# Every two-operand operation that a planner shares out between VectorE and GpSimd goes to VectorE

## The chip, the cores and the metric

The kernel runs on one core of one Trainium2 chip. The metric is the time of one execution on the device in microseconds (us); lower is better. Engines are named as in the profile: PE is TensorE, DVE is VectorE, ACT is ScalarE, POOL is GpSimd, SP the queue that issues most transfers.

## What is computed

Two layers of a transformer trunk over 512 latent tokens and 256 context tokens, width 1024, all in float32. Layer 0 mixes with two kinds of attention over latents (a window, and a 2-D neighbourhood with bias), each latent also reading all context keys; layer 1 with multi-head latent attention (low-rank queries, keys and values, a separate rotary part). Each layer ends in a squared-ReLU MLP of width 4096. Cut to what matters:

```
for i in range(2):
    sh1, sc1, g1, sh2, sc2, g2 = split(silu(c) @ ada_w[i] + ada_b[i], 6)
    h_lat = rms_norm(x, norm_mix[i]) * (1 + sc1) + sh1          # the same for ctx with c_ctx
    y_lat, y_ctx = even_mixer(h_lat, h_ctx, ...) if i % 2 == 0 else odd_mixer(h_lat, h_ctx, ...)
    x = x + g1 * y_lat
    h2 = rms_norm(x, norm_mlp[i]) * (1 + sc2) + sh2
    x = x + g2 * (square(relu(h2 @ mlp_w1[i])) @ mlp_w2[i])     # ctx too in layer 0
return x
```

## The kernel before

**Arithmetic.** A float32 product is made of three fp32r products. An operand is split into a high part (a copy to fp32r: names wh, hh, uh, oh) and a low part, source minus high part (wl, hl, ul, ol); `mm3` adds wh·h, wh·l and wl·h in PSUM. So each weight tile of 128x1024 that arrives by DMA (raw) needs one copy and one subtraction before PE can use it: `split`, called by `Weights.pump` for 128 tiles of the MLPs (wl_w) and for those of the projections (wl_qa, wl_kqb, wl_vb, wl_eo, wl_oi, wl_kv, wl_uq, wl_oo). There are three buffers each for raw, high and low tiles. `split` also makes the low parts of the MLP's activations (ul), of the attention outputs (ol, oh, D) and of latent factors (lr, kb).

**Stages.** Up to 50 us the first modulation; from 50 to about 410 us the first layer's attention (`mixer0`, tiles with _a, _b, _qa, _kqb, _vb in their names); then its output projection (ps_eo) and MLP, to 1060 us; from 1060 to 1390 us the second layer's attention (`mixer1`: 8 pairs of heads, four query jobs `UQ` and eight key-and-value jobs `KV`; tiles with _c, _kv, _uq); then ps_oo and the second MLP. In the MLPs the order is fixed by loops. In the attention stages generators (gemms, their preparation, scores, values, projection) are interleaved by `weave`, which keeps a model of each engine's clock (`Clock`) and always continues the generator whose next PE work could begin first by that model. The schedule is manual: every engine runs its instructions in exactly the order in which this host program emits them, so an instruction that waits holds back all behind it on its engine.

**Who does what.** Three helpers choose an engine by that model when an operation is emitted. `pick` sends a copy to ACT or DVE, `square` a square to ACT or POOL, and `pick2` an operation with two operands in SBUF to POOL or DVE, whichever would end first. `pick2` serves the subtraction in `split` (unless an engine is given, as for three early weight tiles), `scale_by` (normalised queries and keys times 1/rms: ur, oT, qr, kr) and one multiplication by a gain (rows_sb). Other uses of POOL are written out: six additions of squares per norm (nsq). In an attention score half, DVE finds row maxima (mx) and combines them (nm, 128x2), ACT takes the exponential (P), PE transposes P (pp) and multiplies by the values (o).

Of the kernel before, what the change touches and what calls it, by code (L numbers as in the profile page):

```python
# [272 lines left out]
def hybrid_block(  # L273
# [32 lines left out]
    pe, act, dve, pool = (Engine(e, n, ck) for e, n in (  # L306
        (nc.tensor, "pe"), (nc.scalar, "act"), (nc.vector, "dve"), (nc.gpsimd, "pool")))
# [133 lines left out]
    def pick2(n):  # L441

        d = ck.t["dve"] + 0.07 + n / 960
        p = ck.t["pool"] + 0.3 + 2.3 * n / 1000
        return pool if p < d else dve

    def split(hi, lo, src, eng=None):
        copy(hi, src, False)
        (eng or pick2(src.free_size())).tensor_tensor(lo, src, hi.bitcast(F32), op=ALU.subtract)
# [518 lines left out]
    def scale_by(r, y):  # L968

        pick2(r.free_size()).tensor_tensor(r, r, y[:, :, None].to_broadcast(list(r.shape)), op=ALU.mult)  # L970
# [13 lines left out]
    def mixer0(hh, hl, ap, oT, proj, first):  # L984
# [24 lines left out]
        class Unit(Job):  # L1009
# [37 lines left out]
            def prep(self, M):  # L1047
# [17 lines left out]
                for b in range(3):  # L1065
                    scale_by(hd(self.r[b]), box[0][:, b * n2:(b + 1) * n2])
                    if grow is not None:
                        x = hd(self.r[b])
                        pick2(x.free_size()).tensor_tensor(x, x, grow[:, None, :].to_broadcast(list(x.shape)),
                                                           op=ALU.mult)  # L1070
# [1162 lines left out]
```

## Time and profile before

| | |
|---|---|
| time, median of 3 runs | 1787.21 us (1785.69 to 1788.28) |
| the profiled execution's own time | 1784.65 us |
| its span | 1782.8 us |
| PE busy | 1713.3 us, 96% of the span |
| DVE busy | 1030.3 us, 58%, 1908 instructions |
| ACT busy | 653.6 us, 37% |
| POOL busy | 454.3 us, 25%, 241 instructions |

The profile gives the busy time of each engine, and the same by stretches of time. PE's share is an average of stages: in the MLPs it is busy without a break, in the two attention stages it is not. Each group of instructions has a count, a mean duration and the idle time of its engine just before it. An instruction's duration here includes time in which it has begun and is held up by another engine's access.

### The profile page before, as it was taken

The page shows a single profiled execution, that of the slowest core. Times are in us where ns is not written, and L with a number is a line of the kernel's source. Part 1 is how long each engine was busy: PE and PEld are TensorE (multiplying, and loading weights), DVE is VectorE, ACT ScalarE, POOL GpSimd, SP SyncE. Part 2 cuts the span into 40 slices and gives each one's busy share as a digit, 9 for nine tenths or more (in the row PEclk, how much of TensorE's full clock was granted, in tenths as well). Part 3 has the DMA queues.
Part 4 walks back from the last instruction along what each step waited for, and adds up shares of the span by engine and source line. Part 5 has one row for each costly group of instructions (what it writes and reads, how often), then busy time and mean ns, then how long its engine had stood idle before and what let it go on. Part 6 is the DMA issues. An engine that isn't in the chain of part 4 may idle for free. (4 is left out here: it accounts for less than half of the span.)

```text
span 1782.8 us, 27692 instructions
## 1 busy us (share of the span) xinstructions
PE 1713.3 (96%) x11304; PEld 1471.5 (83%) x11304; DVE 1030.3 (58%) x1908; ACT 653.6 (37%) x1403; POOL 454.3 (25%) x241
## 2 busy tenths in 40 slices
PE   9999998989999999999999997999999999999999
PEld 7987876858888888888888896777676898989897
DVE  6767766474667686444445557868864652414242
ACT  3445555343232132132132233555554241414141
POOL 0232111021233332333333222302110233242422
PEclk9999999999999999999999998999999999999999
DMA  9311113043324334343342210001000233323332
GB/s 304 112 60 60 37 48 125 28 142 118 95 84 134 126 118 151 122 130 119 129 127 86 80 47 31 26 1 36 24 13 1 83 107 95 94 90 94 93 94 83
DMA packets 49663, 158.21 MB, mean 89 GB/s; under 512 B 7777, under 2 KB 10209, under 8 KB 49409
## 3 DMA queue, kind: packets, MB, share of 16 engines
q1 hardware_dynamic: 48192, 154.96, 27.4%
q8 instruction: 89, 1.46, 0.3%
q10 hardware_dynamic: 1344, 1.49, 0.3%
q14 instruction: 38, 0.30, 0.1%
HBM read 154.32 MB, written 2.11 MB: 88 GB/s over the span
## 5 line engine op out<-in xcount | busy, mean ns | idle before, releaser
L131 PE MATMUL p<-hh_m,wh_w 128*128 128x258 f32 (+2 forms) x1024 | 317.9, 310 | 0.3 <-DVE fr_m L131 0.3
L131 PE MATMUL p<-hl_m,wh_w 128*128 128x258 f32 (+2 forms) x1024 | 317.9, 310 | 0.0
L131 PE MATMUL p<-hh_m,wl_w 128*128 128x258 f32 (+2 forms) x1024 | 317.7, 310 | 0.0
L131 PE MATMUL p<-ul,wh_w 128*128 128x512 f32 (+1 forms) x768 | 273.1, 356 | 0.0
L131 PE MATMUL p<-uh,wh_w 128*128 128x512 f32 (+1 forms) x768 | 272.2, 354 | 0.0
L131 PE MATMUL p<-uh,wl_w 128*128 128x512 f32 (+1 forms) x768 | 271.7, 354 | 0.0
L131 ACT ACTIVATE wh_w<-raw_w 128x1024 fp32r<-128x1024 f32 x114 | 120.1, 1058 | 397.7 <-PE p L131 383.7
L131 POOL TENSOR_TENSOR wl_w<-raw_w,wh_w 128x1024 fp32r<-128x1024 f32 x65 | 164.9, 2538 | 318.3 <-ACT wh_w L131 263.4
L131 PEld LDWEIGHTS p<-hh_m,wl_w 128*128 128x128 f32 x1024 | 193.4, 189 | 11.1
L131 PEld LDWEIGHTS p<-hh_m,wh_w 128*128 128x128 f32 x1024 | 192.9, 188 | 11.7 <-DVE fr_m L131 0.5
L131 PEld LDWEIGHTS p<-hl_m,wh_w 128*128 128x128 f32 x1024 | 193.1, 189 | 11.2
L131 DVE SCALAR_TENSOR_TENSOR dots<-dot_raw,dots 128x1024 f32<-128x1024 f32 x80 | 148.1, 1851 | 39.6 <-DMA dot_raw<-in_ada_t_dram 38.7
L131 DVE SCALAR_TENSOR_TENSOR x<-p,mod,x 128x512 f32<-128x512 f32 x96 | 60.3, 658 | 189.0 <-PE p L131 189.0
L131 POOL TENSOR_TENSOR ul<-u,uh 128x512 fp32r<-128x512 f32 (+1 forms) x52 | 99.6, 1916 | 258.6 <-DVE uh L131 258.6
L131 PEld LDWEIGHTS p<-uh,wh_w 128*128 128x128 f32 x768 | 145.2, 189 | 21.2
L131 PEld LDWEIGHTS p<-uh,wl_w 128*128 128x128 f32 x768 | 145.0, 189 | 20.9
L131 PEld LDWEIGHTS p<-ul,wh_w 128*128 128x128 f32 x768 | 145.1, 189 | 20.7 <-DVE ul L131 0.2
L131 DVE TENSOR_TENSOR wl_w<-raw_w,wh_w 128x1024 fp32r<-128x1024 f32 x63 | 96.7, 1536 | 100.7 <-ACT wh_w L131 100.4
L131 DVE CAST uh<-u 128x768 fp32r<-128x768 f32 (+1 forms) x64 | 32.7, 510 | 97.7 <-ACT u L131 97.7
L131 ACT ACTIVATE r<-r,bs_p 128x256 f32<-128x256 f32 x64 | 39.5, 617 | 103.9 <-DVE r L131 101.1
L131 PEld LDWEIGHTS pp_c<-ident,P 128*128 128x128 f32 x384 | 46.7, 151 | 26.6 <-issue 14.6
L131 PE MATMUL pp_c<-ident,P 128*128 128x128 f32 x384 | 58.3, 296 | 7.9 <-DVE kb L131 3.1
(494 smaller groups left out, 3472.3 us busy)
## 6 DMA issues: line engine op xcount, KB each, us to landing
raw_w<-in_mlp_w_dram SPq DMA_DIRECT2D x128, 512.0 KB, 3.6
dot_raw<-in_ada_t_dram SPq DMA_DIRECT2D x56, 512.0 KB, 3.7
ada_raw<-in_ada_w_dram SPq DMA_DIRECT2D x24, 512.0 KB, 4.5
ada_raw<-in_ada_s_dram SPq DMA_DIRECT2D x16, 512.0 KB, 10.2
raw_kqb<-in_e_w_in_dram SPq DMA_DIRECT2D x8, 512.0 KB, 3.6
raw_eo<-in_e_w_out_dram SPq DMA_DIRECT2D x8, 512.0 KB, 4.0
raw_oo<-in_o_w_out_dram SPq DMA_DIRECT2D x8, 512.0 KB, 3.4
raw_oi<-in_o_w_in_dram SPq DMA_DIRECT2D x6, 512.0 KB, 3.6
```

Source lines behind the costliest of these rows:

```text
L131: r = f(*a, **k)
```

## The change

`pick2` returns DVE whatever its model says. The model's two estimates are still worked out and no longer used.

```
@@ -442,7 +442,7 @@
 
         d = ck.t["dve"] + 0.07 + n / 960
         p = ck.t["pool"] + 0.3 + 2.3 * n / 1000
-        return pool if p < d else dve
+        return dve
 
     def split(hi, lo, src, eng=None):
         copy(hi, src, False)
```

In the order of the instructions this takes 195 operations from POOL to DVE. In the second attention stage after 1080 us they are 32: 13 scalings qr (8 of 512 columns, 5 of 256), 7 scalings kr (768), 5 wl_kv (3 of 896, 2 of 512), 2 wl_oo (1024), 4 low parts of the attention output (512) and kb (768). In the first one, between 50 and 410 us, they are 35: 14 weight splits (1024), 4 ol (768), 17 scalings (15 of 512, 2 of 256). Most of the others are in the MLPs (65 wl_w and 52 ul). POOL keeps the 18 norm additions and the squares. Because `weave`, `pick` and `square` read the model's clocks, other things move with it: 41 single-operand copies go from DVE to ACT, and 12 squares from ACT to POOL (24 squares there before, 36 now). In the second attention stage these are 22 copies, net, and 8 squares (8 before, 16 now); in the first about 12 copies and 4 squares (16 before, 20 now). PE runs the same instructions; in the first attention stage they come in a visibly different order, in the second nearly in the same one.

DVE at the opening of the second attention stage, where the raw queries of the first `UQ` job (two tiles qr, each 128x768 with 8 heads of 64 plain and 32 rotary columns) are multiplied by 1/rms (y) and rotated (tu). Before:

```order
L131 TENSOR_TENSOR y_uq_10411<-y_uq_10404,w_uq_10407 128x32
L131 TENSOR_TENSOR qr_uq_10154<-qr_uq_10154,y_uq_10411 128x8x32
L131 TENSOR_TENSOR qr_uq_10154<-qr_uq_10154,rows_sb 128x8x32
L131 TENSOR_TENSOR tu_uq_10416<-qr_uq_10154,ropeq 128x256
L131 TENSOR_TENSOR tu_uq_10416<-qr_uq_10154,ropeq 128x16x8 x2
L131 TENSOR_TENSOR qr_uq_10154<-tu_uq_10416 128x8x32
L131 TENSOR_TENSOR qr_uq_10196<-qr_uq_10196,rows_sb 128x8x32
L131 TENSOR_TENSOR tu_uq_10424<-qr_uq_10196,ropeq 128x256
```

The same place now:

```order
L131 TENSOR_TENSOR y_uq_10411<-y_uq_10404,w_uq_10407 128x32
L131 TENSOR_TENSOR qr_uq_10154<-qr_uq_10154,y_uq_10411 128x8x64
L131 TENSOR_TENSOR qr_uq_10154<-qr_uq_10154,y_uq_10411 128x8x32
L131 TENSOR_TENSOR qr_uq_10154<-qr_uq_10154,rows_sb 128x8x32
L131 TENSOR_TENSOR tu_uq_10416<-qr_uq_10154,ropeq 128x256
L131 TENSOR_TENSOR tu_uq_10416<-qr_uq_10154,ropeq 128x16x8 x2
L131 TENSOR_TENSOR qr_uq_10154<-tu_uq_10416 128x8x32
L131 TENSOR_TENSOR qr_uq_10196<-qr_uq_10196,y_uq_10411 128x8x64
L131 TENSOR_TENSOR qr_uq_10196<-qr_uq_10196,y_uq_10411 128x8x32
L131 TENSOR_TENSOR qr_uq_10196<-qr_uq_10196,rows_sb 128x8x32
L131 TENSOR_TENSOR tu_uq_10424<-qr_uq_10196,ropeq 128x256
```

Three multiplications by y that POOL did beside DVE now stand in DVE's own row, two of them with 8x64 columns per partition.

DVE late in the first attention stage, at the last normalisation of neighbourhood queries and keys (three tiles ur_kqb; w and y are the steps to 1/rms), between the first tiles of the output projection (wl_eo, oh, ol) and a piece of the modulation (mod). Before:

```order
L131 TENSOR_TENSOR w_kqb_4317<-y_kqb_4305 128x24
L131 TENSOR_TENSOR w_kqb_4317<-w_kqb_4317,v_kqb_4300 128x24
L131 TENSOR_SCALAR w_kqb_4317<-w_kqb_4317 128x24
L131 TENSOR_TENSOR y_kqb_4321<-y_kqb_4305,w_kqb_4317 128x24
L131 CAST oh_4356<-oT 128x768
L131 TENSOR_TENSOR ol_4357<-oT,oh_4356 128x768
L131 TENSOR_TENSOR ur_kqb_4075<-ur_kqb_4075,y_kqb_4321 128x512
L131 TENSOR_TENSOR ur_kqb_4209<-ur_kqb_4209,y_kqb_4321 128x512
L131 TENSOR_TENSOR wl_eo_4384<-raw_eo_4315,wh_eo_4383 128x1024
L131 TENSOR_TENSOR mod_107<-ada_pt_4391,adab_sb 128x16 x2
L131 TENSOR_TENSOR ol_4357<-oT,oh_4356 128x768
L131 SCALAR_TENSOR_TENSOR k_kqb_4372<-ut_kqb_4415,gains_sb,k_kqb_4371 64x512
```

The same place now:

```order
L131 TENSOR_TENSOR wl_eo_4288<-raw_eo_4243,wh_eo_4287 128x1024
L131 TENSOR_TENSOR w_kqb_4293<-y_kqb_4281 128x24
L131 TENSOR_TENSOR w_kqb_4293<-w_kqb_4293,v_kqb_4276 128x24
L131 TENSOR_SCALAR w_kqb_4293<-w_kqb_4293 128x24
L131 TENSOR_TENSOR y_kqb_4297<-y_kqb_4281,w_kqb_4293 128x24
L131 TENSOR_TENSOR ur_kqb_3977<-ur_kqb_3977,y_kqb_4297 128x512
L131 TENSOR_TENSOR ur_kqb_4168<-ur_kqb_4168,y_kqb_4297 128x512
L131 TENSOR_TENSOR ur_kqb_4257<-ur_kqb_4257,y_kqb_4297 128x512
L131 TENSOR_TENSOR ol_4340<-oT,oh_4339 128x768 x2
L131 SCALAR_TENSOR_TENSOR k_kqb_4336<-ut_kqb_4359,gains_sb,k_kqb_4335 64x512
```

The weight split wl_eo, the third scaling and the low parts ol that POOL did are now in DVE's row; the three scalings stand right behind y, and the modulation no longer stands between them and the transposed keys (k_kqb<-ut_kqb).

POOL through the first three groups of jobs of the second attention stage, 143 to 150 of its row before, sq being squares:

```order
L131 TENSOR_TENSOR sq_uq_10691<-qr_uq_10376 128x768
L131 TENSOR_TENSOR sq_uq_10695<-qr_uq_10542 128x768
L131 TENSOR_TENSOR wl_kv_10704<-raw_kv_10323,wh_kv_10703 128x512
L131 TENSOR_TENSOR qr_uq_10376<-qr_uq_10376,y_uq_10769 128x8x64
L131 TENSOR_TENSOR qr_uq_10376<-qr_uq_10376,y_uq_10769 128x8x32
L131 TENSOR_TENSOR qr_uq_10542<-qr_uq_10542,y_uq_10769 128x8x64
L131 TENSOR_TENSOR qr_uq_10542<-qr_uq_10542,y_uq_10769 128x8x32
L131 TENSOR_TENSOR sq_kv_10864<-kr_kv_10580 128x768
```

The same jobs now:

```order
L131 TENSOR_TENSOR sq_kv_10429<-kr_kv_10248 128x768
L131 TENSOR_TENSOR sq_kv_10485<-kr_kv_10328 128x768
L131 TENSOR_TENSOR sq_uq_10608<-qr_uq_10381 128x768
L131 TENSOR_TENSOR sq_uq_10627<-qr_uq_10545 128x768
L131 TENSOR_TENSOR sq_kv_10878<-kr_kv_10586 128x768
```

Only squares are left there, among them those of KV jobs that ACT did before.

## Rows read from the trace of the kernel before

**Rows 1.** The view by stretches: start and end in us, length, then busy us (and instructions) of PE, PE's weight loads, DVE, ACT and POOL, granted PE clock as a share of full speed, DMA share and GB/s.

```profile
50.00:410.00 360.00, 332.43 (x2708) 275.52 (x2707) 248.17 (x585) 169.63 (x512) 77.17 (x51) 0.99 0.23 73
410.00:1060.00 650.00, 649.09 (x3806) 572.79 (x3805) 371.78 (x530) 174.94 (x242) 197.51 (x78) 1.00 0.36 114
1080.00:1390.00 310.00, 279.92 (x1849) 218.35 (x1849) 217.31 (x463) 161.21 (x428) 54.21 (x39) 0.93 0.06 18
1390.00:1783.00 393.00, 388.98 (x2439) 351.93 (x2438) 144.94 (x236) 120.34 (x173) 120.94 (x66) 1.00 0.31 94
```

**Rows 2.** The chain that ended last, by engine as shares of the span, and its first piece (start us, us, what).

```profile
PE 34%; DVE 4%; ACT 1%; issue 0%; ACTq 0%
...
1079.85 1.49 PE st_kr L131 x12
```

**Rows 3.** Groups of POOL instructions between 1080 and 1390 us: count, busy us, mean ns, then POOL's idle time before them and what ended it.

```profile
L131 POOL TENSOR_TENSOR qr_uq<-qr_uq,y_uq 128x512 f32<-128x512 f32 (+1 forms) x13 | 11.6, 923 | 18.2 <-DVE y_uq L131 18.2
L131 POOL TENSOR_TENSOR kr_kv<-kr_kv,y_kv 128x768 f32<-128x768 f32 x7 | 10.3, 1473 | 57.6 <-DVE y_kv L131 57.6
L131 POOL TENSOR_TENSOR wl_kv<-raw_kv,wh_kv 128x896 fp32r<-128x896 f32 (+1 forms) x5 | 8.9, 1781 | 64.3 <-ACT wh_kv L131 51.0 <-DVE wh_kv L131 13.2
L131 POOL TENSOR_TENSOR sq_uq<-qr_uq 128x768 f32<-128x768 f32 x4 | 6.5, 1644 | 0.1
...
L131 POOL TENSOR_TENSOR sq_kv<-kr_kv 128x768 f32<-128x768 f32 x3 | 4.6, 1521 | 13.4 <-DVE kr_kv L131 8.2 <-DVE qr_uq L131 5.3
```

**Rows 4.** The same for POOL between 50 and 410 us.

```profile
L131 POOL TENSOR_TENSOR wl_kqb<-raw_kqb,wh_kqb 128x1024 fp32r<-128x1024 f32 x8 | 19.0, 2376 | 50.0 <-DVE wh_kqb L131 24.2 <-ACT wh_kqb L131 15.1 <-issue 10.6
L131 POOL TENSOR_TENSOR ur_kqb<-ur_kqb,y_kqb 128x512 f32<-128x512 f32 x8 | 8.6, 1098 | 24.9 <-DVE y_kqb L131 24.9
```

**Rows 5.** Groups of DVE instructions in the second attention stage, 1080 to 1390 us, columns as above.

```profile
L131 DVE COPY P<-pp_c 128x512 f32<-128x512 f32 x36 | 24.8, 688 | 28.5 <-PE pp_c L131 28.5
...
L131 DVE TENSOR_TENSOR nm_c<-mx_c 128x2 f32<-128x2 f32 x32 | 11.1, 347 | 1.1
...
L131 DVE TENSOR_TENSOR tu_uq<-qr_uq,ropeq 128x256 f32<-128x256 f32 x8 | 6.4, 802 | 0.3
...
L131 DVE TENSOR_TENSOR qr_uq<-tu_uq 128x256 f32<-128x256 f32 x8 | 3.4, 424 | 0.3
...
L131 DVE TENSOR_TENSOR wl_oo<-raw_oo,wh_oo 128x1024 fp32r<-128x1024 f32 x2 | 2.4, 1224 | 0.1
...
L131 DVE TENSOR_TENSOR w_kv<-y_kv 128x12 f32<-128x12 f32 x7 | 1.1, 160 | 0.0
...
L131 DVE TENSOR_TENSOR wl_kv<-raw_kv,wh_kv 128x512 fp32r<-128x512 f32 x1 | 0.7, 692 | 0.0
```

**Rows 6.** Groups of DVE instructions in the stretch of the first MLP, 410 to 1060 us.

```profile
L131 DVE SCALAR_TENSOR_TENSOR dots<-dot_raw,dots 128x1024 f32<-128x1024 f32 x80 | 148.1, 1851 | 39.6 <-DMA dot_raw<-in_ada_t_dram 38.7
...
L131 DVE TENSOR_TENSOR ul<-u,uh 128x768 fp32r<-128x768 f32 x8 | 7.7, 959 | 0.3
```

**Rows 7.** Instructions in order of time at 1125 us, POOL and DVE: start us, us, what, count, idle time before and what ended it.

```profile
1125.37 2.13 POOL L131 TENSOR_TENSOR wl_kv<-raw_kv,wh_kv 128x896 fp32r<-128x896 f32 x1 [10.22 <-ACT wh_kv L131]
...
1125.63 1.87 DVE L131 TENSOR_TENSOR nm_c<-mx_c 128x2 f32<-128x2 f32 x1
```

**Rows 8.** DVE and POOL at the opening of the second attention stage in order of time (the durations of merged rows run over all of them), PE there, and the stretch around it in the columns of Rows 1.

```profile
1100.11 3.21 POOL L131 TENSOR_TENSOR qr_uq<-qr_uq,y_uq 128x512 f32<-128x512 f32 x3 [4.97 <-DVE y_uq L131]
1100.52 1.15 DVE L131 TENSOR_TENSOR qr_uq<-qr_uq,rows_sb 128x256 f32<-128x256 f32 x1
1101.70 1.97 DVE L131 TENSOR_TENSOR tu_uq<-qr_uq,ropeq 128x256 f32<-128x256 f32 x3
...
1104.27 0.63 PE L131 MATMUL qt_uq<-ident,qr_uq 128*96 128x128 f32 x2 [6.18 <-DVE qr_uq L131]
...
1104.50 0.83 DVE L131 TENSOR_TENSOR tu_uq<-qr_uq,ropeq 128x256 f32<-128x256 f32 x3
...
1098.00:1122.00 24.00, 14.64 (x53) 11.42 (x53) 15.45 (x36) 9.05 (x22) 4.68 (x4) 0.64 0.00 0
```

**Rows 9.** POOL, DVE and PE late in the first attention stage in order of time, and the stretch from 360 to 380 us.

```profile
363.74 2.40 POOL L131 TENSOR_TENSOR wl_eo<-raw_eo,wh_eo 128x1024 fp32r<-128x1024 f32 x1 [3.48 <-DVE wh_eo L131]
...
363.79 2.39 DVE L131 TENSOR_TENSOR w_kqb<-w_kqb,v_kqb 128x24 f32<-128x24 f32 x1
...
368.23 3.77 DVE L131 TENSOR_TENSOR ur_kqb<-ur_kqb,y_kqb 128x512 f32<-128x512 f32 x2
...
371.92 2.82 DVE L131 TENSOR_TENSOR wl_eo<-raw_eo,wh_eo 128x1024 fp32r<-128x1024 f32 x1
...
375.06 0.63 PE L131 MATMUL ut_kqb<-ident,ur_kqb 128*128 128x128 f32 x4 [3.34 <-DVE mod L131]
...
360.00:380.00 20.00, 16.06 (x99) 12.12 (x98) 16.81 (x21) 7.11 (x12) 7.98 (x5) 0.91 0.42 133
```

**Rows 10.** Two groups of DVE instructions between 50 and 410 us.

```profile
L131 DVE TENSOR_TENSOR wl_qa<-raw_qa,wh_qa 128x1024 fp32r<-128x1024 f32 x2 | 4.3, 2132 | 0.0
...
L131 DVE TENSOR_TENSOR w_qa<-y_qa 128x24 f32<-128x24 f32 x2 | 2.3, 1148 | 0.9 <-ACT y_qa L131 0.9
```

**Rows 11.** DVE's waits for ACT in the same stretch: us in total, times, longest.

```profile
DVE wl_eo L131 <- ACT wh_eo L131: 4.1, 1, 4.1
...
DVE wl_vb L131 <- ACT wh_vb L131: 2.5, 1, 2.5
```

More of the change, by code (lines that the diff above doesn't have):

```diff
@@ L444, in pick2 @@
         p = ck.t["pool"] + 0.3 + 2.3 * n / 1000
-        return pool if p < d else dve
+        return dve
     def split(hi, lo, src, eng=None):
```

## The prediction

> **What bounds the kernel now.** I read the view by stretches first, then the chain that ended last, then the groups of POOL and DVE with their idle times, and last the order of time at the places named. From 410 to 1060 us PE is busy 649.1 of 650 us, from 1390 to the end 389.0 of 393 [rows 1]: in the output projections and MLPs nothing counts but PE. In the attention stages it does not run through: 27.6 of 360 us idle in the first, 30.1 of 310 in the second, where the granted clock averages 0.93, so some of the time runs at the lower level of 1.2 GHz. The change can act in these 670 us only. The chain view reaches back to 1079.85 us and gives DVE 4% of the span and ACT 1% [rows 2]: 71 and 18 us, nearly all in the second attention stage, as PE holds the rest behind it. DVE is busy 217.3 us there [rows 1], so a microsecond of DVE work has so far been on the path in 71/217 = 0.33 of cases.
>
> **What a moved operation costs on DVE.** Where nothing disturbs it, DVE needs 1.22 us for 1024 columns, 0.96 for 768, 0.69 for 512 and 0.42 for 256 [rows 5, 6]; for 896 I estimate 1.09 between its neighbours. POOL needs 2.38 for 1024, 1.47 for 768, 1.10 for 512 [rows 3, 4]: about 1.5 to 2 times as long, but beside DVE, not in its row.
>
> **What it gives back.** A POOL operation is not free for DVE. At 1125.37 us POOL starts a split of 2.13 us, and DVE's nm_c, 128x2, begins at 1125.63 and ends with it after 1.87 us [rows 7]; the small products of this size take 0.16 [rows 5]. Over the stage the 32 nm_c average 347 ns and the 8 tu_uq of 256 columns 802 ns against 424 for their sister [rows 5]: 32 x 0.187 + 8 x 0.378 = 9.0 us of held-up DVE per 54.2 us of POOL [rows 1], 0.17 us each. The MLP shows the same: dots of 1024 columns at 1.85 us [rows 6].
>
> **The MLPs and projections: 0.** Even if POOL's whole time there went to DVE at POOL's length, DVE would have 371.8 + 197.5 = 569 of 650 us and 144.9 + 120.9 = 266 of 393 [rows 1], and it is really half of that, less what dots gets back. PE covers it. DVE's splits will wait in its row for ACT's high parts, with evacuations of PSUM queued behind; DVE already makes some of the splits there, and PE doesn't stop. Bounds -1 to +3 us.
>
> **The second attention stage: +4.6.** The 32 operations add to DVE: qr 8 x 0.69 + 5 x 0.42 = 7.6; kr 7 x 0.96 = 6.7; wl_kv 3 x 1.09 + 2 x 0.69 = 4.7; wl_oo 2 x 1.22 = 2.4; output parts 4 x 0.69 = 2.8; kb 0.96: together 25.1. Taken off: 22 copies go to ACT, between 0.42 and 0.69 each [rows 5], at most 15 and, most of them small, some 10. ACT, busy 161 of 310 [rows 1], gives up 8 squares for them and stays where it is. Held-up time: POOL loses the 43.1 us that aren't squares (54.2 less sq_uq 6.5 and sq_kv 4.6 [rows 3]), worth 7.3; its squares double, +11.1 us, which costs 1.9; net 5.4 given back. New waits: a moved split stands in DVE's row until ACT has the high part; on POOL that was free (wl_kv waited 51.0 us for ACT [rows 3]). Of 11 splits that DVE makes in the attention stages two waited, 4.1 and 2.5 us [rows 11], the others hardly, see wl_oo, wl_kv and wl_qa [rows 5, 10]: 0.6 each, 7 splits, 4.2. Net 25.1 - 10 - 5.4 + 4.2 = 13.9 us on DVE, x 0.33 = +4.6. The ends: none of it on the path and the held-up time all on it, -5.4; all of it on the path, +14.
>
> At its opening I expect nothing. PE idles 6.18 us for qr_uq and then runs at a clock of 0.64 over 24 us [rows 8]. POOL's three scalings (3.21 us) become 2 x 0.69 + 0.42 = 1.8 us on DVE; back come 1.15 - 0.42 and 1.97 - 0.83 = 1.9 us there [rows 8]. A wash, and the gap remains long enough for the lower clock.
>
> **The first attention stage: +3.3.** Added: 14 x 1.22 + 4 x 0.96 + 15 x 0.69 + 2 x 0.42 = 32.1 us. No chain reaches this stage; I scale by idle PE per busy DVE, 27.6/248.2 = 0.111 against 30.1/217.3 = 0.139 [rows 1]: 0.33 x 0.8 = 0.26. One place is priced by itself. At 363.74 us a POOL split holds w_kqb for 2.39 instead of 0.16, then POOL's ol and ur lengthen two scalings to 3.77 from 1.38, and ol wl_eo to 2.82 from 1.22; PE idles 3.34 us and the clock falls, 0.91 over 20 us [rows 9]. That is 6.2 us held up; in its place wl_eo, two ol and one ur, 1.22 + 2 x 0.96 + 0.69 = 3.8, stand in the row: -2.4, all on the path, and -1.0 for the clock (0.09 x 20 = 1.8 us lost, half of it returned): -3.4. The rest: 32.1 - 3.8 = 28.3 added; waits 14 x 0.6 = 8.4; about 12 copies to ACT at 0.42, -5; other held-up time -6 (wl_qa 2 x 0.91 and w_qa 2 x 0.99 [rows 10] are 3.8 of it; the rest of this is scattered): 25.7 x 0.26 = +6.7. Less 3.4: +3.3. Ends: -8 (the idle 3.34 us and the 1.8 us of clock gone, 3 more from the rest) to +12 (0.6 on the path). The order of PE's work is also redrawn here, which I can't price; it is why the ends are wide.
>
> **The sum.** 0 + 4.6 + 3.3 = +8 us on the profiled execution's own time of 1784.65 us (span 1782.8): 1792.6. That execution lies 2.6 us below the median of the runs, 1787.2, so a median is forecast at 1795.
>
> A rule on which the two views pull apart: the Trainium skill, Perfetto Trace Analysis, section Optimizing Scalar/DVE Operations, says that handing work to GpSimd may make sense where DVE is saturated, though it might not help, as the two share a read port into SBUF. By its first half, taking the hand-over back costs where DVE is fullest, as my sum has it; by its second half it costs nothing and the time stays at 1787. DVE at 217 of 310 us is neither full nor idle, and the trace shows both halves at work.
>
> **The rivals.** *Faster, 1775.* DVE has 93 of 310 and 112 of 360 us idle [rows 1], and the planner may place the added work in these, while every held-up nm and w stands just ahead of something PE wants. Then 5.4 us return in the second stage and 8 at the upper end of the first, together 12 to 13. It decides once less than a fifth of what DVE gains (25.1 + 32.1 - 15 of copies = 42 us, so 8) is on the path against half of what was held up (5.4 + 6 + 6.2 = 17.6 us). For it: nm_c [rows 7] and the place at 364 us [rows 9]. Against: no row of DVE is reordered by the hardware, so work that is emitted between y and the transposes stands in front of them. Chance 0.27. The Trainium skill, GPSIMD Engine Reference, section 4.1 Engine selection, puts elementwise work on VectorE because GpSimd takes about twice as long with two inputs; 2.38 against 1.22 us agrees, and by that rule alone this rival wins.
>
> *No change, 1787.* Gains at 364 us and losses elsewhere cancel, since the plan is made anew with the load shifted to ACT. Chance 0.21.
>
> *Much slower, 1810.* From 1100 us on DVE becomes the limit: with all of 13.9 and half of 25.7 us on the path, 13.9 + 12.9 - 3.4 = 23 us; new PE gaps, each followed by time at 1.2 GHz (0.64 over 24 us is 8.6 us of clock lost [rows 8]), could carry it further. It decides once DVE passes some 80% in the middle of the stage. Chance 0.12.
>
> **How the numbers follow.** The forecast, slower by 4 to 15 us, has 0.40; with the much slower case 0.52 for slower by over 0.2% (3.6 us, about what a measurement of this kernel tells from no change), 0.21 within it, 0.27 faster. The likeliest is 1795, its own range 1790 to 1803. For 8 in 10 the range reaches to the faster case and past the slower one: 1776 to 1813.
>
> **What would show it.** POOL falls from 454 to some 90 us and DVE rises from 1030 to about 1090, dots towards 1.22 us, the price of 1024 columns alone; 410 to 1060 and 1390 to the end unchanged within 3 us. In the second stage nm_c nearer 0.2 us, DVE some 5% busier, PE idle 33 to 38 us of a longer stage; in the first PE's 3.34 us before ut_kqb gone, more small gaps before. The forecast is wrong if PE's idle time falls in both stages (the faster case), or if the stretch of either MLP changes by more than 3 us.

## The result, and the profile after

The changed kernel takes 1810.87 us (median of 4 runs, 1808.83 to 1818.14), the kernel before 1786.45 beside it: a ratio of 1.0143, 95% interval 1.0124 to 1.0161, or +24 us. The forecast was +8 us, a median of 1795.

PE's work is the same, so I cut both traces where PE's work says that a stage begins: up to the first MLP matmul, the MLP, the opening of the second attention stage up to st_kr, from there to the first c_c, from there to the last matmul of the output projection (ps_oo), the rest. First the kernel before, by stretches (start and end, length, then busy us and instructions of PE, PE's weight loads, DVE, ACT and POOL, granted clock, DMA share, GB/s):

```profile
50.00:474.10 424.10, 396.34 (x3086) 330.58 (x3086) 289.96 (x642) 186.78 (x542) 94.64 (x59) 0.99 0.26 82
474.10:1015.10 541.00, 540.66 (x3100) 475.67 (x3099) 308.82 (x425) 140.25 (x180) 167.63 (x64) 1.00 0.37 116
1015.10:1079.80 64.70, 61.12 (x427) 56.69 (x425) 36.31 (x75) 24.36 (x47) 16.70 (x9) 1.00 0.17 52
1079.80:1107.30 27.50, 20.25 (x127) 17.91 (x127) 20.50 (x48) 10.98 (x16) 8.66 (x6) 0.86 0.13 41
1107.30:1417.30 310.00, 287.09 (x1842) 222.85 (x1842) 219.14 (x439) 157.98 (x424) 54.64 (x39) 0.94 0.07 23
1417.30:1782.00 364.70, 361.71 (x2321) 329.68 (x2319) 122.61 (x212) 112.78 (x160) 111.86 (x60) 1.00 0.31 94
```

The same stretches of the changed kernel:

```profile
50.00:481.70 431.70, 400.81 (x3083) 333.46 (x3081) 300.11 (x666) 192.71 (x550) 34.84 (x26) 0.97 0.25 81
481.70:1022.50 540.80, 540.56 (x3100) 475.79 (x3099) 310.02 (x481) 142.56 (x182) 13.57 (x6) 1.00 0.38 116
1022.50:1093.50 71.00, 64.71 (x428) 59.10 (x427) 38.95 (x83) 25.12 (x48) 2.94 (x2) 0.95 0.16 48
1093.50:1121.40 27.90, 20.29 (x127) 17.87 (x128) 21.20 (x47) 11.91 (x20) 4.57 (x3) 0.84 0.12 41
1121.40:1443.80 322.40, 288.63 (x1841) 223.34 (x1841) 227.29 (x454) 163.42 (x436) 24.50 (x18) 0.93 0.08 23
1443.80:1809.00 365.20, 361.77 (x2321) 329.70 (x2320) 163.65 (x264) 116.32 (x163) 0.97 (x1) 1.00 0.30 93
```

Read down the lengths: +7.6 us to the first MLP matmul, 0 in the MLP, +6.3 in the opening, +0.4, +12.4 in the rest of the second attention stage, the last stretch the same but for where I cut it. In the +12.4 PE's busy time hardly grows (+1.5): its idle time does, from 22.9 to 33.8 us, while DVE's busy time grows by 8.2 and is only 70% of the stretch (227.3 of 322.4).

What was held up by POOL did come back. Groups of DVE instructions, count, busy us, mean ns, idle before; the first two in the second attention stage, the third in the stretch of the first MLP, which answer to [rows 5, 6]:

```profile
L131 DVE TENSOR_TENSOR nm_c<-mx_c 128x2 f32<-128x2 f32 x32 | 5.2, 161 | 1.1
L131 DVE TENSOR_TENSOR qr_uq<-qr_uq,y_uq 128x512 f32<-128x512 f32 (+1 forms) x16 | 12.0, 790 | 0.0
L131 DVE SCALAR_TENSOR_TENSOR dots<-dot_raw,dots 128x1024 f32<-128x1024 f32 x80 | 97.7, 1221 | 12.3 <-DMA dot_raw<-in_ada_t_dram 11.4
```

nm_c falls from 347 to 161 ns, dots from 1851 to 1221; the stage still got longer. In the first stretch and the opening something else is to be read, too: PE needs longer for the same matmuls, 4.5 of the 7.6 us and 3.6 of the 6.3, at granted clocks of 0.97 and 0.95 instead of 0.99 and 1.00; the rest is idle time.

The longest new gap shows what such a loss looks like. DVE, POOL, ACT and PE in order of time (start us, us, what, count, idle time before and what ended it):

```profile
1222.32 1.02 DVE L131 TENSOR_TENSOR qr_uq<-qr_uq,y_uq 128x512 f32<-128x512 f32 x2
...
1225.04 2.29 DVE L131 TENSOR_TENSOR qr_uq<-qr_uq,y_uq 128x512 f32<-128x512 f32 x2
...
1229.02 0.74 DVE L131 SCALAR_TENSOR_TENSOR kb<-kt_kv,gains_sb,kb 64x512 fp32r<-64x512 f32 x1
...
1225.29 1.76 POOL L131 TENSOR_TENSOR sq_kv<-kr_kv 128x768 f32<-128x768 f32 x1 [15.81 <-DVE qr_uq L131]
...
1224.34 0.69 ACT L131 ACTIVATE kb<-kt_kv,gains_sb 64x512 fp32r<-64x512 f32 x1
1229.80 1.18 ACT L131 ACTIVATE kb<-kt_kv,gains_sb 64x512 fp32r<-64x512 f32 x2 [4.77 <-DVE kb L131]
...
1232.31 1.09 ACT L131 ACTIVATE P<-pp_c 128x512 f32<-128x512 f32 x2
...
1232.96 1.12 PE L131 MATMUL pp_c<-ident,P 128*128 128x128 f32 x4 [6.53 <-ACT P L131]
...
1228.00:1240.00 12.00, 7.04 (x36) 4.99 (x36) 6.00 (x13) 5.73 (x10) 0.00 (x0) 0.57 0.00 1
```

From 1222.32 to 1229.0 DVE scales and rotates two query tiles; behind that stands kb, the low part of the keys. ACT's next kb waits for DVE's, 4.77 us, and ACT's copy of P, for which PE waits, stands behind it in ACT's row: PE is idle 6.53 us, and over the 12 us from 1228 the granted clock averages 0.57, so in part it was the lower level of 1.2 GHz. Three things make the block: the new order puts it ahead of kb, the scalings (1.02 us a pair undisturbed) are now in DVE's row, and the second pair takes 2.29 while a square of 1.76 us runs on POOL. The order weighs most here: kernel 6 below has it with three of the four scalings back on POOL, and the same wait is 8.69 us.

The opening is a stretch for which the prediction had no term of its own. PE and DVE of the changed kernel, then POOL before:

```profile
1079.27 0.41 PE L131 MATMUL g_uq<-wh_uq,lr 128*128 128x384 f32 x1 [2.14 <-DVE lr L131]
1081.23 0.45 PE L131 MATMUL g_uq<-wh_uq,lr 128*128 128x384 f32 x1 [0.88 <-ACT lr L131]
...
1076.72 0.69 DVE L131 TENSOR_TENSOR wl_kv<-raw_kv,wh_kv 128x512 fp32r<-128x512 f32 x1 [0.81 <-ACT wh_kv L131]
1077.33 0.69 DVE L131 TENSOR_TENSOR kr_t<-g_oi,fr_a 128x512 f32<-128x512 f32 x1
1077.93 0.74 DVE L131 SCALAR_TENSOR_TENSOR zt<-zt,gains_sb,lr_oi 128x512 f32<-128x512 f32 x1
1078.70 0.43 DVE L131 CAST lr<-zt 128x512 fp32r<-128x512 f32 x1
1079.16 0.69 DVE L131 TENSOR_TENSOR lr<-zt,lr 128x512 fp32r<-128x512 f32 x1
```

```profile
1066.41 1.52 POOL L131 TENSOR_TENSOR lr<-zt,lr 128x512 fp32r<-128x512 f32 x1 [4.03 <-ACT lr L131]
1069.89 1.29 POOL L131 TENSOR_TENSOR lr<-zt,lr 128x512 fp32r<-128x512 f32 x1 [1.95 <-ACT lr L131]
```

The latent factors are multiplied (zt), copied (lr) and their low part taken, one 512 columns after the other. Before, POOL took low parts while DVE went on; now DVE does, with a weight split, for which it waits 0.81 us, ahead of all of it. Here too the order has a part of its own: in kernel 6, where POOL takes low parts again and the same weight split still stands ahead on DVE, the opening is as long and PE waits 2.20 us at the same matmul.

### The profile page after: what moved, and what is told of

Its sections match the earlier page's. It is cut to its first block, busy times and chain, and to the rows that moved or that the text cites. A ratio compares the mean times of both kernels' runs of the same rounds, so it can differ in the third digit from the quotient of the medians.

```text
span 1809.4 us, 27541 instructions
## 1 busy us (share of the span) xinstructions
PE 1722.7 (95%) x11304; PEld 1477.3 (82%) x11304; DVE 1094.4 (60%) x2062; ACT 672.5 (37%) x1432; POOL 81.6 (5%) x58
## 4 chain that ended last, share of the span: by engine, by line
PE 85%; DVE 10%; ACT 2%; DMA 1%; issue 1%; ACTq 0%; DVEq 0%
PE p L131 50%; PE ps_eo L131 3%; PE g_kqb L131 3%; PE o_c L131 2%; PE ps_oo L131 2%; PE g_oi L131 2%; PE pp_c L131 2%; PE g_qa L131 2%; PE l_c L131 2%; PE g_kv L131 2%; PE o_a L131 1%; DVE kb L131 1%; PE g_vb L131 1%; PE o_b L131 1%; PE c_c L131 1%; DVE qr_uq L131 1%
## 5 line engine op out<-in xcount | busy, mean ns | idle before, releaser
L131 ACT ACTIVATE wh_w<-raw_w 128x1024 fp32r<-128x1024 f32 x119 | 125.5, 1059 | 444.1 <-PE p L131 444.1
L131 DVE TENSOR_TENSOR wl_w<-raw_w,wh_w 128x1024 fp32r<-128x1024 f32 x128 | 165.7, 1296 | 123.5 <-ACT wh_w L131 113.0
L131 DVE SCALAR_TENSOR_TENSOR dots<-dot_raw,dots 128x1024 f32<-128x1024 f32 x80 | 97.7, 1221 | 12.3 <-DMA dot_raw<-in_ada_t_dram 11.4
L131 ACT ACTIVATE r<-r,bs_p 128x256 f32<-128x256 f32 x64 | 39.5, 617 | 71.4 <-DVE r L131 68.6
L131 ACT ACTIVATE P<-pp_c 128x512 f32<-128x512 f32 x67 | 38.6, 597 | 58.3 <-PE pp_c L131 58.2
L131 PE MATMUL l_c<-kb,D 96*128 96x512 f32 x192 | 59.2, 428 | 0.0
## 6 DMA issues: line engine op xcount, KB each, us to landing
ada_raw<-in_ada_s_dram SPq DMA_DIRECT2D x16, 512.0 KB, 10.7
```

Of the source, the lines that this page charges most:

```text
L131: r = f(*a, **k)
```

## The experiments

**One table first**: for each kernel the median of its runs, and from its profiled execution the three stretches that move: start of the first MLP matmul; from the last MLP matmul to st_kr (opening); from st_kr to the last ps_oo (rest). The MLP itself is 540.8 to 542.0 us in all but kernel 2 (550.9).

| kernel | us | first attention and projection | opening | rest |
|---|---|---|---|---|
| before | 1786 to 1788 | 474.1 | 64.8 | 337.2 |
| changed | 1810.9 | 481.7 | 71.0 | 350.1 |
| 1 old order, 195 on VectorE | 1805.8 | 480.5 | 68.8 | 346.7 |
| 2 new plan, GpSimd by a shadow clock | 1834.5 | 493.9 | 69.6 | 353.4 |
| 3 VectorE in first attention only | 1792.0 | 481.8 | 64.8 | 336.4 |
| 4 VectorE in second attention only | 1809.0 | 477.8 | 71.0 | 351.9 |
| 5 old order, new engines | 1822.7 | 490.8 | 68.6 | 357.6 |
| 6 new order, old engines | 1833.6 | 491.3 | 71.0 | 358.2 |
| 7 old order, scalings on VectorE | 1801.3 | 481.4 | 64.8 | 344.3 |
| 8 old order, low parts on VectorE | 1795.5 | 477.8 | 67.9 | 338.9 |
| 9 old order, new copies | 1810.8 | 490.4 | 64.4 | 348.3 |
| 10 old order, new squares | 1791.2 | 481.0 | 64.8 | 336.6 |
| 11 changed, modulation first | 1825.3 | 490.8 | 71.0 | 351.8 |
| 12 as 3, modulation first | 1802.2 | 491.6 | 64.8 | 335.7 |
| 13 old rule, other plan (0.17) | 1790.4 | 480.0 | 64.9 | 336.0 |
| 14 old rule, other plan (0.23) | 1795.7 | 487.3 | 64.7 | 336.2 |
| 15 rule for scalings alone | 1808.4 | 478.3 | 64.8 | 354.1 |
| 16 rule for low parts alone | 1801.1 | 494.3 | 72.3 | 323.4 |
| 17 changed rule, other plan (0.26) | 1812.3 | 483.7 | 71.0 | 349.5 |
| 18 old rule, other plan (0.26) | 1795.0 | 481.7 | 64.8 | 335.8 |

Where the instructions of the second attention stage are the same, bar a few at most (before, 3, 12 to 14, 18; changed, 4, 11, 17), opening and rest repeat within 2.4 us. The first column is less sure: kernel 4 has the rows of the kernel before there and stands at 477.8, 1.9 of the 3.7 us lost before 77 us. So a loss of 4 us in this column can be chance.

**Theories.** A: the moved work stands in VectorE's in-order row ahead of what PE waits for. B: the planner, reading a fuller VectorE clock, writes another order of PE's work, and that order costs.

**1 and 2: one without the other.** In the first the planner books the work as POOL's, so order and all other choices stay; in the second it books VectorE and POOL does it.

```
+    dve_as_pool = Engine(nc.vector, "pool", ck)
...
-        return pool if p < d else dve
+        return dve_as_pool if p < d else dve
```

```
+    pool_as_dve = Engine(nc.gpsimd, "dve", ck)
+    shadow = [0.0]
...
+        p = max(shadow[0], ck.t["pool"]) + 0.3 + 2.3 * n / 1000
+        if p < d:
+            shadow[0] = max(shadow[0], ck.t["dve"]) + 0.14 + 2.17 * n / 1000
+            return pool_as_dve
+        return dve
```

> Order and choices of the kernel before kept to the letter (PE, ACT and SP rows are the same as before); only the 195 operations that POOL did are issued on VectorE instead, noted in the planner as POOL work. Theory A (the moved work in DVE's in-order row delays what PE waits for): as slow as the changed kernel or more, 1806 to 1820 us, since here DVE doesn't even give 41 copies to ACT; the opening of the second attention stage, its rest and the first attention stage all longer. Theory B (the planner, reading a fuller VectorE clock, made another order of PE's work and of copies and squares, and that order costs the time): 1785 to 1791, as before; PE's gap of 6.5 us that the changed kernel has near 1230 us is missing.

> The reverse: the plan of the changed kernel (rows of PE, ACT and SP the same as its rows, 41 copies on ACT, squares on POOL), but about 195 two-operand operations run on GpSimd as before, chosen by the old rule with a POOL clock of their own. Theory A: back to 1780 to 1790 us, the gap of 6.5 us near 1230 gone. Theory B: 1805 to 1814, with the filler matmuls of the opening and the waits for modulation weights (ada_ps) as in the changed kernel.

Measured: 1805.8 (ratio 1.011, 1.008 to 1.014) and 1834.5 (1.0281, 1.0251 to 1.0311). The first is just below A's range and far above B's: with PE's order kept the work alone costs 19 us. Neither theory has the second: the new order with POOL at work is worse than either kernel, and at the place of the changed kernel's gap of 6.53 us PE still waits 5.28. Its choice by a shadow clock isn't that of the kernel before, so run 6 repeats it exactly.

**3 and 4: by stage.** The rule holds only while a stage is planned (`stage[0]` set ahead of each).

```
-        return pool if p < d else dve
+        return dve if stage[0] in ("a0",) else pool if p < d else dve     # 4: ("a1",)
```

> VectorE alone in the first attention stage with its projection, the old rule after that. The trace puts 7.6 us of the loss there. If the stages add up: 1792 to 1797 us. If something later depends on it (the plan of a stage starts from where the one before left the clocks): another time, the first MLP matmul still 7 to 8 us later.

> VectorE alone in the second attention stage only, the old rule elsewhere. The trace puts 6.3 us (opening) and 12.9 us (rest) there: 1803 to 1808 us if the stages add up. The remainder, MLPs, should be worth nothing: with the run for the first attention stage the two should sum to the whole +24 us within 3.

1792.0 (1.0025, 1.0012 to 1.0038) and 1809.0 (1.0129, 1.0105 to 1.0154): they add up to 27.8 us, where the whole is 24.4; a little over the 3 us of difference that were expected. Kernel 4 lies 1 us above its range, with 3.7 us in the first stage, where its rows are those of the kernel before. The second attention stage is worth four fifths of it, the MLPs nothing.

**5 and 6: the other two corners.** A table, taken from both plans, gives each copy, high part, low part, scaling, gain and square its engine, and the planner books it where its own plan has it; so order and engines are exchanged exactly.

```
+    def real(plan, kind, a):
+        k = key(kind, a)
+        e = ISSUE.get(k, plan.name)
+        n = {"act": nc.scalar, "dve": nc.vector, "pool": nc.gpsimd}[e]
+        return e, Engine(n, plan.name, ck)
...
-        (eng or pick2(src.free_size())).tensor_tensor(lo, src, hi.bitcast(F32), op=ALU.subtract)
+        (eng or real(pick2(src.free_size()), "low", lo)[1]).tensor_tensor(lo, src, hi.bitcast(F32), op=ALU.subtract)
```

> Order of the kernel before (PE and SP rows the same as its rows), but each copy, high part, low part, scaling, gain and square is issued on the engine that the changed kernel gives it: 195 operations from GpSimd to VectorE, net 41 copies from VectorE to ScalarE, 12 squares from ScalarE to GpSimd. So far: the 195 alone cost +19 us in this order, order and engines of the changed kernel together +24. Theory A (the moved work in VectorE's row): the copies relieve VectorE, +8 to +17, 1795 to 1804 us. Theory B (the new order of PE): the cost of engines alone, no more than +8, up to 1795. Theory C (order and engines are made for each other, any mixture is worse): above 1811.

> The fourth corner: order of the changed kernel (PE and SP rows the same as its rows), every one of those operations on the engine that the kernel before gives it, GpSimd again with its 195. Theory A: 1780 to 1793 us. Theory B: 1806 to 1816, the order being what costs. Theory C: above 1811; the run of the new order with GpSimd chosen by a shadow clock (1834) points to C.

1822.7 (1.0199, 1.0177 to 1.0221) and 1833.6 (1.0263, 1.0241 to 1.0285). Theory C: order and engines are made for each other. B falls as it stood (in the old order the engines cost 36 us), and A alone can't explain that the new order with POOL back costs 47. Given the new engines, the new order saves 12 us. The place of the 6.53 us gap, in kernel 6:

```profile
1236.62 3.16 POOL L131 TENSOR_TENSOR qr_uq<-qr_uq,y_uq 128x512 f32<-128x512 f32 x3
...
1235.89 1.05 DVE L131 TENSOR_TENSOR qr_uq<-qr_uq,y_uq 128x256 f32<-128x256 f32 x1
...
1244.08 0.74 DVE L131 SCALAR_TENSOR_TENSOR kb<-kt_kv,gains_sb,kb 64x512 fp32r<-64x512 f32 x1
...
1248.08 1.11 PE L131 MATMUL pp_c<-ident,P 128*128 128x128 f32 x4 [8.69 <-ACT P L131]
```

The two query tiles stand ahead of kb as in the changed kernel, with POOL beside DVE, and the wait is longer. So that gap belongs to the new order and not to the scalings alone. The text ahead of the prediction calls PE's order in the second attention stage nearly the same; compared row by row, by names and shapes, 242 of its 2394 matmuls from the last MLP matmul to the last ps_oo stand elsewhere, a tenth, hardly less than in the first stage (428 of 3494). The next four kernels therefore keep the order of the kernel before.

**7 and 8: which of the 195.** The same table with one kind in it: 37 scalings and gains, or 158 low parts.

```
+ISSUE = {k: "dve" for k in moved if k.split()[0] in ("scale", "gain")}     # 8: ("low",)
```

> Order and engines of the kernel before, only the 37 scalings and gains (all in the attention stages) moved from GpSimd to VectorE. Theory A1 (blocks of scalings stand in VectorE's row ahead of what PE waits for): most of the +19, 1797 to 1806 us. Theory A2 (low parts do it, which wait in the row for ScalarE's high part): 1784 to 1792.

> Order and engines of the kernel before, only the 158 low parts (weight splits, attention output, MLP inputs, kb) moved from GpSimd to VectorE. Theory A1: 1785 to 1793 us. Theory A2: 1797 to 1806, with VectorE waiting for ScalarE's high parts. With the run of the scalings the two should sum to about +19 if they act in different places.

1801.3 (1.008, 1.0054 to 1.0105) and 1795.5 (1.0052, 1.0035 to 1.0068). The scalings cost more, and in the rest of the second attention stage they are nearly all of it (+7.1 of 8.8 for both); the low parts make the opening (+3.1 of 4.0 in run 1, where the scalings make none). Kernel 7 is as A1 expected; kernel 8 lies between the two ranges, and the two sum to 23 us, not 19. A1 and A2 each hold in a different place. With the order kept, a place can be laid over itself. Kernel 7, DVE, POOL and PE:

```profile
1157.90 1.03 DVE L131 TENSOR_TENSOR qr_uq<-qr_uq,y_uq 128x512 f32<-128x512 f32 x2
...
1160.63 2.29 DVE L131 TENSOR_TENSOR qr_uq<-qr_uq,y_uq 128x512 f32<-128x512 f32 x2
...
1164.27 0.42 DVE L131 TENSOR_TENSOR qr_uq<-tu_uq 128x256 f32<-128x256 f32 x1
...
1160.85 1.79 POOL L131 TENSOR_TENSOR sq_kv<-kr_kv 128x768 f32<-128x768 f32 x1 [11.94 <-DVE qr_uq L131]
...
1164.75 0.98 PE L131 MATMUL qt_uq<-ident,qr_uq 128*96 128x128 f32 x6 [2.13 <-DVE qr_uq L131]
```

The kernel before at the same instructions:

```profile
1142.53 3.19 POOL L131 TENSOR_TENSOR qr_uq<-qr_uq,y_uq 128x512 f32<-128x512 f32 x4 [4.56 <-DVE y_uq L131]
...
1146.95 0.43 DVE L131 TENSOR_TENSOR qr_uq<-qr_uq,rows_sb 128x256 f32<-128x256 f32 x1
...
1151.08 0.42 DVE L131 TENSOR_TENSOR qr_uq<-tu_uq 128x256 f32<-128x256 f32 x1
...
1151.65 0.83 PE L131 MATMUL qt_uq<-ident,qr_uq 128*96 128x128 f32 x6 [0.59 <-DVE qr_uq L131]
```

With four scalings in it the block takes DVE 6.79 us, before 4.55, as POOL had done them earlier beside DVE; PE waits 2.13 instead of 0.59, and 0.6 in each of the other kernels with the rows of the kernel before: 1.5 us for four scalings. Such places add up, though not every wait is a clean price. At kernel 7's longest, 5.25 us for P at 1298 us, the kernel before waits 2.17, but 1.10 to 3.77 in the others with its rows, as the clock sets how early PE arrives there; laid over from the matmuls before, this place costs 0.7 us.

**9 and 10: what the plan moves along.** The table with the copies and high parts alone (96 from VectorE to ScalarE, 55 the other way), or with the 12 squares alone.

> Order of the kernel before, GpSimd keeps its 195 operations and ScalarE its squares; only the copies and high parts go where the changed kernel puts them (96 from VectorE to ScalarE, 55 the other way). In the old order all new engines cost +36 us, the 195 alone +19, so copies and squares add 17. If the copies do that by themselves (ScalarE's row, with the copies of P that PE waits for, gets work at places that the order didn't count on): 1799 to 1808 us. If they only hurt beside the 195: 1785 to 1793. My prediction had them as relief of VectorE: 1779 to 1785.

> Order of the kernel before with one thing changed: the 12 squares that the changed kernel moves from ScalarE to GpSimd. If GpSimd's squares (some 1.5 us each where ScalarE needs less) hold up VectorE and come late for the sums: 1790 to 1797 us. If they are covered: 1785 to 1790.

1810.8 (1.0151, 1.0126 to 1.0177) and 1791.2 (1.0025, 1.0011 to 1.0040). The first is above all that was expected. In the old order the new copies cost as much as the whole change: they take DVE's busy time in the rest of the second stage from 219 to 211 us, and the stage is longer all the same. An order made for other engines is part of that price. The squares cost at most the 5 us, none of it in the second attention stage.

**11 and 12: a remedy that failed.** At 310 us PE has 13 of the 24 modulation pieces (ada_ps) left in the changed kernel, 9 in the kernel before. In the projection it then waits for their DMAs:

```profile
399.63 1.08 PE L131 MATMUL ada_ps<-ada_raw,sT 128*32 128x256 f32 x8 [2.72 <-DMA ada_raw<-in_ada_w_dram]
...
411.06 0.64 PE L131 MATMUL ada_ps<-ada_raw,sT 128*32 128x256 f32 x8 [2.14 <-DMA ada_raw<-in_ada_w_dram]
```

```
-        weave(ck, [masks(), biases(), spare(), ...
+        weave(ck, [chain(ada_stream(A, M, PT, [(1, 2), (2, 1)], 2), lend(A, M, 1, lambda: True)),
+                   masks(), biases(), spare(), ...
```

> The changed kernel with the modulation pieces (ada_ps) offered to the planner first instead of last, so that they are done long before the output projection of the first attention stage. If the new order loses its 8.5 us in that projection because 13 of 24 pieces are left and PE waits for their DMAs: 6 to 9 us faster than the changed kernel, 1802 to 1805, no wait for ada_raw after 365 us. If these pieces were only filling gaps that something else causes, the time goes into the attention proper: 1807 to 1814.

> The same remedy in the kernel with VectorE alone in the first attention stage only, where ps_eo began 0.9 us earlier than in the kernel before and the loss came behind it. If the pieces explain it: 1783 to 1786 us, level with the kernel before or a little better. If not: 1788 to 1795.

1825.3 (1.0228, 1.0202 to 1.0255) and 1802.2 (1.0104, 1.0075 to 1.0132): 14 and 10 us worse than without, outside every range. The projection did get shorter, from ps_eo to the MLP 100.9 us instead of 115.1 in the changed kernel, but ps_eo begins at 389.9 instead of 366.6. The pieces had been filling gaps; offered first, they are run where their data isn't there yet (kernel 11, PE's waits from 50 to 490 us: total, times, longest; 6.5 in 5 in the changed kernel):

```profile
PE ada_ps L131 <- DMA ada_raw<-in_ada_w_dram: 9.2, 12, 1.3
```

**13, 14, 18 and 17: is any other plan worse?** Theory D: the kernel before simply has a good plan. The constant in `pick` is changed, and the rest follows:

```
-        a = ck.t["act"] + 0.19 + n / 1200
+        a = ck.t["act"] + 0.17 + n / 1200     # 14: 0.23; 18: 0.26; 17: 0.26 in the changed kernel
```

> The kernel before with one constant of the planner changed, 0.19 to 0.17 us for ScalarE in the choice between ScalarE and VectorE for a copy. The plan comes out otherwise (some 3,000 lines of difference in PE's rows, 8 more operations on ScalarE, 5 fewer on GpSimd), but VectorE gets no two-operand work. Theory A (VectorE's added work costs): within 4 us of the kernel before, 1783 to 1791. Theory D (any other plan is worse; the one of before is a lucky one): 1795 to 1812.

> The same with 0.23: another plan with the same division of work (5 operations from GpSimd to ScalarE). Theory A: 1783 to 1791 us. Theory D: 1795 to 1812.

> The kernel before with the same constant at 0.26: a third plan under its rule (some 3,300 lines of difference in PE's rows), GpSimd keeping 242 operations. From the two others: 1788 to 1798 us. At 1803 or more the spread of plans would be as wide as the whole effect.

> The changed kernel with the planner's constant 0.19 set to 0.26: another plan (some 1,000 lines of difference in PE's rows), all 195 operations on VectorE. If the rule sets the level: 1805 to 1818 us. If the changed kernel's plan is an unlucky one: 1790 to 1803.

Old rule: 1790.4 (1.0023, 1.0012 to 1.0033), 1795.7 (1.0046, 1.0029 to 1.0062) and 1795.0 (1.0037, 1.0023 to 1.0051). Changed rule: 1812.3 (1.0143, 1.0114 to 1.0173). Theories A and D are each right in part. Other plans of the old rule lose 4 to 8 us, all of it in the first attention stage: from the second on their PE and DVE rows are those of the kernel before. The changed rule stays where it was. In its second stage kernel 17 differs from the changed kernel by a handful of rows, so on another plan of that stage these four say nothing.

**15 and 16: planned halves.** `pick2` returns DVE for scalings and gains alone, or for low parts alone.

```
-    def pick2(n):
+    def pick2(n, low=False):
...
-        return pool if p < d else dve
+        return pool if low and p < d else dve     # 16: if not low and p < d
```

> The rule changed for scalings and gains alone (about 37 operations always on VectorE), low parts still by the old rule, plan made accordingly. Theory A: 10 to 16 us over the kernel before, as when the scalings moved in the old order (+14): 1797 to 1803. Theory D: anything from 1790 to 1812, with losses in places that hold no scaling.

> The rule changed for low parts alone (about 158 always on VectorE), scalings by the old rule, plan made accordingly. Theory A: 5 to 11 us over the kernel before (+8.5 in the old order): 1791 to 1797. Theory D: anything from 1790 to 1812.

1808.4 (1.0119, 1.0098 to 1.0139) and 1801.1 (1.0077, 1.0061 to 1.0093), both above what A expected. In the second attention stage (opening and rest) the scalings alone cost 16.9 us; the low parts alone save 6.3, although their opening is the longest of all; they lose it again in the first stage (494.3). Waits of PE in the rest of that stage, kernel 15 first, then 16:

```profile
PE pp_c L131 <- ACT P L131: 6.5, 1, 6.5
PE pp_c L131 <- ACT x L131: 5.9, 1, 5.9
```

```profile
PE c_c L131 <- ACT P L131: 11.2, 8, 2.6
PE qt_uq L131 <- DVE qr_uq L131: 2.7, 2, 2.1
```

In kernel 15 both gaps stand behind a block of two scaled and rotated query tiles ahead of kb, the first at an earlier job than in the changed kernel; in kernel 16 no wait of PE is longer than 2.6 us. What kernel 16 gains from the first c_c on is not idle time, though:

```profile
1129.90:1430.80 300.90, 277.91 (x1840) 214.54 (x1841) 222.90 (x443) 160.18 (x430) 42.88 (x34) 0.98 0.08 25
```

PE idles 23.0 us, as before (22.9), and does the same matmuls in 277.9 us instead of 287.1, at a granted clock of 0.98 instead of 0.94. A kernel with the first attention of the kernel before and the second of kernel 16 would be 6 us faster by these stretches of one execution; it was not run.

## Why the prediction was wrong

**Right:** MLPs and projections at 0 (the MLPs within 1 us); POOL's busy time to 81.6 us (454 before) and DVE's to 1094; in the rest of the second stage 8.2 us more DVE work, where the sum had 9.7 without the waits for high parts; dots at 1.22 us; nm_c at 0.16; the gap of 3.34 us before ut_kqb gone; the 24 us at 1098 to 1122 a wash (27.5 and 27.9 us from st_kr to c_c).

**The term of the second attention stage, +4.6, was mis-sized: 12.4 us.** The step that failed is "x 0.33". It took the share of DVE's work that had been on the path as the share that more work would be on. With the order kept, DVE's busy time in the rest of the stage grows from 219.1 to 233.0 us and the stretch by 9.1: 0.66. That 13.9 is also the forecast's net is chance, as kernel 1 gives no copies to ACT. The rows of kernels 1, 7 and 8:

```profile
1119.20:1438.30 319.10, 287.55 (x1841) 222.40 (x1841) 233.00 (x468) 158.95 (x426) 16.86 (x11) 0.94 0.07 23
1115.70:1431.60 315.90, 286.36 (x1842) 221.74 (x1842) 228.23 (x456) 157.83 (x424) 37.45 (x22) 0.94 0.07 23
1116.10:1426.80 310.70, 284.97 (x1842) 220.25 (x1842) 224.80 (x451) 158.92 (x426) 35.01 (x28) 0.95 0.07 24
```

Scalings alone add 9.1 us to DVE and 5.9 to the stretch (0.65); low parts add 5.7 to DVE and 0.7 to the stretch, which is within what equal rows vary by. So the added work is not a sample of DVE's work. A scaling stands in one block with the rotation, directly ahead of PE's transposes or of kb and so of ACT's row; a microsecond there is on the path more often than DVE's average microsecond. The order made for the changed rule adds the rest of the 12.4; PE's idle time from st_kr to the last ps_oo is 41 us, forecast 33 to 38.

**"Taken off: 22 copies go to ACT" was no relief.** In the changed kernel DVE carries 5.7 us less in this stretch than in kernel 1 (227.3 and 233.0) and the stretch is 3.3 longer. The new copies alone, in the old order, lengthen the stage by 10.7 us (kernel 9). More than half of PE's waiting from the first c_c on ends with ACT's work on P (18.8 of 33.6 us in the changed kernel), so work handed to ACT goes into a row that PE waits for; which copies do it was not taken apart, and that it is the copies in the new order too isn't shown. That ACT "stays where it is" in busy time was true (163 us) and said nothing.

**"At its opening I expect nothing" priced the wrong stretch.** It looked at 1098 to 1122 us, which is a wash. Of the stretch from 1015 to 1080 I had counted all up to 1060 to the MLP's, where PE runs without a break, and the last 20 us to nothing; it holds low parts of lr and weight splits that POOL did for DVE (eight, 15.2 us busy), and it lost 6.3 us. With the order kept the low parts cost 3.1 of it and the scalings nothing; the new order has 69.6 to 71.0, whichever engine does the work.

**The clock** stood in the sum with -1.0 at one place, half of what was lost there returned. It fell instead: PE's busy time grew by 4.5 us up to the first MLP matmul, 3.6 in the opening and 1.5 in the rest, 9.6 of the 26.6 us by which the profiled execution is longer.

**First attention stage, +3.3 against +7.6: not settled.** The gap before ut_kqb closed as priced, and ps_eo begins 0.9 us earlier than before (366.6 and 367.5). The loss is behind it, in the projection, where PE waits for modulation weights. But other plans of the old rule lose as much in this stage (480.0 to 487.3 against 474.1, and against 477.8 in kernel 4, whose rows there are those of the kernel before), and the remedy failed. That more work on VectorE is the cause here isn't shown.

**The rivals.** The faster one fell: held-up time came back, in nm_c all of it, and counted for little. *Much slower, 1810* has the time, though not by its condition: DVE is 70% busy, not over 80%. Gaps followed by time at 1.2 GHz came without it. *No change* counted on the plan made anew to cancel losses; beside the work with the order kept (kernel 1) the new plan adds 5 us. The sentence of the Trainium skill on saturation (Perfetto Trace Analysis, Optimizing Scalar/DVE Operations) didn't decide it; the one at the end of that section, on engines that aren't saturated but cause bubbles on others, describes what the trace shows, DVE at 70% and 10.9 us more idle time of PE.

**How much is what.** The second attention stage (opening and rest) is 19.1 us longer in the changed kernel. By way of kernel 1, 13.5 of it is the moved work with the order kept (scalings 7.1 and low parts 4.8 apart, in kernels 7 and 8), and the remaining 5.6 belongs to the plan made around it; whether to its copies or to PE's order stays open. By way of kernel 6 the shares come out otherwise: the new order with the old engines is 27.2 us longer, and the new engines give 8.1 back. So the runs show what the rule costs and that the moved work costs in the old order; in the new one, with POOL at work again (kernels 2 and 6), the stage is longer still, and no single share is the moved work's. The other 7.6 us are in the first stage, 5.4 by the median of kernel 3, about as much as each other plan of the old rule lost there (5.9 to 13.2).

## What to carry to other kernels

Price an operation that is moved to another engine's row by what stands directly behind it in that row and who waits for that, not by the engine's busy share or by the average share of its work on the path. Lay a wait over itself in several executions before taking it for a price: PE's clock alone moved one from 1.10 to 3.77 us. Where a planner reads clocks, exchange order and engines separately before blaming either, and run two or three plans that differ only in a harmless constant: here they lost 4 to 8 us by themselves. Of the work that two engines could do, try the kinds apart: here the scalings cost on VectorE with the order kept (14 us) and with a new plan (22 us). The low parts cost 8 us with the order kept; in one new plan the second attention stage was 6 us shorter with them on VectorE, much of it by PE's clock, and that kernel as a whole was 14 us slower.

## What the runs showed of the hardware that was not expected

A square on POOL, one tensor read as both operands, goes with a held-up VectorE as a split does: at 1225 us two scalings took 2.29 us instead of 1.02 while a square of 1.76 us ran beside them. I had valued POOL's time at 0.17 us of hold-up per us; at this one place it was 1.27 us for 1.76, just ahead of the longest gap of the kernel. Kernel 7 has the same 2.29 us at 1160.63, beside a square of 1.79.
